# Float32 products of the gated heads' decay and gate rows, replaced by float32r products on stacked rows, in a two-branch recurrent block

## The chip, the cores and the metric

The kernel runs on one core of one Trainium2 chip. The metric is the device time of one execution in microseconds (us); lower is better. A core has five engines with a queue of instructions each: TensorE (PE, matrix products), VectorE (DVE), ScalarE (ACT), GpSimd (POOL) and SyncE (SP, which here issues the loads). Each queue runs in order, and engines wait for each other by semaphores.

## The reference, cut to what matters

One layer: a modulated RMSNorm of 512 latent and 256 context tokens of width 2048, two groups of four heads (gated linear attention, "GLA", and mLSTM) over all tokens in both directions, an output projection, and a gated feed-forward part with a 3x3 convolution. The part that the change touches is the decay of the GLA heads and the gate rows of the mLSTM heads:

```
z = einsum('btd,dp->btp', h, w_in)          # 16 columns are glr, 16 are mgate
dec = einsum('btr,zrk->zbtk', glr, gla_w_lr) + gla_b_lr[:, None, None, :]
gla_loga = log_sigmoid(dec) / 16            # per direction, token, head and 128 channels
pre = mgate.reshape(b, t, 2, 2, 4) + mlstm_b_gate
ml_logi, ml_logf = pre[:, :, :, 0], log_sigmoid(pre[:, :, :, 1])
```

The scans then use the cumulative sums of `gla_loga` within and across chunks. All of it is float32.

## The kernel before, in words

Large products are made exact enough from float32r, a form in which an operand of a product is rounded: each operand is split into a rounded part `hi` and the rest `lo` (`split`: ACT casts, DVE subtracts), and three products are summed (`mm3`, recorded in `mm`, line 95). Small products are plain float32.

The kernel first projects heads 0 and 1 (`project_first`) while the modulation rows `ps_m` are made by products with the loaded `w_mod`. Then come the 32 low-rank rows: `gm` sums them in four strips of 32 partitions, and `small_rows` adds the strips with two products and copies 16 rows to partitions 0 to 15 and 16 rows to 32 to 47 of the tile `glr`, which was set to 1.0 before, so that partition 16 holds ones for the bias.

Then, for each head h, the work of head h (`gla` or `mlstm`, written as generators that yield how many microseconds of other PE work they want) is woven with the projection of head h + 1 (`project_steps`): `weave` takes as many projection steps as the yields ask for. PE's order is pinned to the order of recording, so it is this interleaving that sets what PE does next. In `gla`, nine levels `lv` each make `ex` (DVE differences, ACT exponentials, DVE product with q and k), a product `sl` on PE, and a masked copy of `sl` into `sc` (DVE). After some of these levels, `next(after, None)` records one step of the next head's preparation, `gla_prep(h + 1)`:
- two steps `dec`, one for each direction: PE product of 17 rows, `log_sigmoid` (three ACT operations in `lt`, a DVE operation to `la`);
- two steps `cdec`, for the context tokens: two PE products of 128 columns each, `log_sigmoid` through `ct` to `cla`;
- one step with the scans `bt` (DVE) and the sums `csum` (PE, from `cla`);
- one with `b2` and `ends`.

Head 0's preparation has no levels to stand between and runs in `first_stages` with yields written there. The PSUM tiles of all these small products come from a pool of two (`psb`). After the last GLA head, `ml_gates` picks the gate rows out of `glr` with products by columns of the identity (`pre`), 4 rows for each direction, kinds i and f, latent and context.

Of the kernel before, what the change touches and what calls it, by code (L numbers as in the profile page):

```python
# [11 lines left out]
F32 = mybir.dt.float32  # L12
F32R = mybir.dt.float32r
# [5 lines left out]
P = 128  # L19
# [3 lines left out]
T = 512  # L23
TJ = T // P
TC = 256
CJ = TC // P
H = 4
DK = 128
# [14 lines left out]
C_ID, C_LS, C_US, C_SEG = (P * i for i in range(4))  # L43
C_SA = C_SEG + T
# [25 lines left out]
def block_kernel(ctx: ExitStack, tc: tile.TileContext, a: dict, out: bass.AP):  # L70
    nc = tc.nc
# [22 lines left out]
    def mm(*args, **kw):  # L94
        ins = PE.matmul(*args, **kw)  # L95
        if pinned[0]:
            tc.keep_in_program_order(ins)
# [26 lines left out]
    def cc(off, n=P, p=P):  # L124
        return cst[0:p, off : off + n]
# [270 lines left out]
    st_h = ExitStack()  # L396
    states = pool(st_h, "states")

    glr = states.tile([48, T + TC], F32, name="glr")
# [92 lines left out]
    mskf = mraw.tile([P, len(LEVELS), P], F32, name="mskf", tag="raw")  # L492
    nc.sync.dma_start(mskf, a["masks"])
    V.tensor_copy(msk, mskf)

    V.memset(glr, 1.0)
    gm = [ytile(i, f"gm{i}", (P, n)) for i, n in enumerate((T, TC))]
    pinned[0] = True
    for c0, n, hs, m in ((0, T, hx, gm[0]), (T, TC, hc, gm[1])):
# [11 lines left out]

    def small_rows():
        for c0, n, m in ((0, T, gm[0]), (T, TC, gm[1])):
            ps = psb(f"glr{c0}", (48, n))
            mm(ps[0:16, :], cc(C_SA, 16), m, start=True, stop=True)
            mm(ps[32:48, :], cc(C_SA + 16, 16), m, start=True, stop=True)
            V.tensor_copy(glr[0:16, c0 : c0 + n], ps[0:16, :])
            S.copy(glr[32:48, c0 : c0 + n], ps[32:48, :])
            yield 1.4


# [5 lines left out]
    def wtile(name, tag, *shape):  # L527
        return (wkh if tag in ("qk", "v", "kn", "vn") else wk).tile([P, *shape], F32, name=name, tag=tag)
# [44 lines left out]

    def gla_prep(h, out):

        wlr = wk2.tile([17, 2, DK], F32, name=f"wlr{h}", tag="wlr")
        nc.sync.dma_start(wlr, a["w_lr"][h])
        la = wtile(f"la{h}", "la", 2, T)
        t = wtile(f"lt{h}", "tmp", 2, T)
        cla = wtile(f"cla{h}", "cla", 2, CJ, DK)  # L580
        ct = ytile(15, f"ct{h}", (P, 2, CJ, DK))
# [12 lines left out]
        bt = [ytile(8 + d, f"bt{h}{d}") for d in range(2)]  # L594
        for d in range(2):
            o, x = bt[d], la[:, d]
            if d == 1:
                o, x = o[:, ::-1], x[:, ::-1]
            V.tensor_tensor_scan(out=o, data0=cc(C_SEG, T), data1=x, initial=0.0, op0=ALU.mult, op1=ALU.add)

        ps = psb(f"csum{h}", (P, 2, CJ, DK))
        for d in range(2):
            tri = cc(C_LS) if d == 0 else cc(C_US)
            for j in range(CJ):
                more = j == d
                mm(ps[:, d, j, :], tri, cla[:, d, j, :], start=True, stop=not more)
                if more:
                    mm(ps[:, d, j, :], ones, cla[:, d, 1 - j, :], start=False, stop=True)
# [29 lines left out]
    def gla(h, pair, qk, v, kn, vn, yT, prep, fill, after, pending):  # L638
# [12 lines left out]
        for lv, b in enumerate(LEVELS + [P, 2 * P]):  # L651
# [80 lines left out]
    def ml_gates():  # L732
# [142 lines left out]
    def first_stages(tiles):  # L875

        yield from small_rows()
        prep = gla_prep(0, preps[0])
        for need in (0, 1.4, 0, 3, 1, 0):
            next(prep)  # L880
            yield need
        end = yield from gla(0, *tiles, yT, preps[0], 2.2, gla_prep(1, preps[1]), lambda: None)
        q, k, v0, v1, *c = early_sums
        tiles = ([], (q, k), [v[:, b, :] for v in (v0, v1) for b in range(2)],
                 [e[:, 0:DK] for e in c], [e[:, DK:] for e in c])
        end = yield from gla(1, *tiles, yT, preps[1], 2.2, gla_prep(2, preps[2]), end)
        yield 4
        end()
# [251 lines left out]
def arrange(x, c, ctx, c_ctx, w_mod, b_mod, g_norm1, g_norm2, w_in, gla_w_lr, gla_b_lr, mlstm_b_gate,  # L1140
# [31 lines left out]
    lr = np.concatenate([gla_w_lr[0], gla_b_lr[0][:, None, :]], 1)  # L1172
    r["w_lr"] = lr.reshape(2, 17, H, DK).transpose(2, 1, 0, 3)
    bg = np.zeros((36, 2), np.float32)
    for d in range(2):
        bg[32 * d : 32 * d + H] = mlstm_b_gate[0, d].T
# [25 lines left out]
```

## Time and profile before

| what | value |
|---|---|
| time, median of 3 runs (lowest to highest) | 2604.83 us (2601.96 to 2608.07) |
| the profiled execution: span from first to last instruction | 2605.5 us |
| PE busy | 2543.7 us, 98% |
| DVE busy | 1360.2 us, 52% |
| ACT busy | 875.6 us, 34% |
| mean DMA rate over the span | 123 GB/s |

The profiled execution has no time of its own beside its span; the span lies 0.7 us above the median of the runs. A row of the page's table of groups or of one tile's instructions gives line, engine, operation, output<-inputs, count and durations; a row of the timeline begins with the start and the duration in us, and ends in brackets with the idle time of the engine ahead of it and who ended it. The chain of waits gives start, duration and what the time went to, and merges equal neighbours. A float32 product shows as two records on PE, a float32r product as one.

### The profile page before, as it was taken

To read this page: it belongs to the slowest core of one execution; us is meant where nothing else is said; L and a number is where in the kernel's file an instruction comes from. 1 tells how busy PE (TensorE), PEld (TensorE's weight loads), DVE (VectorE), ACT (ScalarE), POOL (GpSimd) and SP (SyncE) were. 2 spreads that over 40 slices of the span, in tenths; PEclk is the share of its full clock that TensorE was granted. 3 is DMA by queue.
4 is the path that set the end of the run, shared out by engine and by line. 5 is a ranking of instruction groups with operands and counts; after the bars stand their busy time and mean duration, and the time that the engine had idled before them with its cause. 6 is when DMAs were issued, how large, how long until landed. Compare 5 with 4: busy or idle time off the path is not lost.

```text
span 2605.5 us, 31876 instructions
## 1 busy us (share of the span) xinstructions
PE 2543.7 (98%) x12822; PEld 2134.9 (82%) x12822; DVE 1360.2 (52%) x1973; ACT 875.6 (34%) x1300; POOL 226.1 (9%) x179
## 2 busy tenths in 40 slices
PE   5999999999999999999999999999999999999998
PEld 3887889888897887878878888888888888888887
DVE  5566765553434466448586336533653365336643
ACT  4224543332324344334343123312331233123431
POOL 0000000111212323210321000000000000000000
PEclk9999999999999999999999999999999999999999
DMA  8851012222333566642654222322232223222421
GB/s 309 294 194 42 33 41 74 73 79 83 122 122 122 194 228 219 198 139 89 209 180 149 98 96 96 97 97 96 97 97 97 97 97 97 97 97 89 142 89 65
DMA packets 96604, 321.37 MB, mean 123 GB/s; under 512 B 11140, under 2 KB 15560, under 8 KB 96456
## 3 DMA queue, kind: packets, MB, share of 16 engines
q1 hardware_dynamic: 95304, 318.82, 35.7%
q8 instruction: 100, 1.64, 0.3%
q10 hardware_dynamic: 1152, 0.52, 0.1%
q14 instruction: 48, 0.39, 0.0%
HBM read 315.10 MB, written 4.19 MB: 123 GB/s over the span
## 4 chain that ended last, share of the span: by engine, by line
PE 89%; DVE 5%; DMA 4%; ACT 1%; issue 1%; POOL 0%; SPq 0%; DVEq 0%; ACTq 0%; POOLq 0%
PE ug L95 17%; PE a L95 17%; PE dn L95 17%; PE uv L95 16%; PE wo L95 6%; PE ga L95 5%; PE po L95 3%; DMA raw_m<-in_w_mod 3%; PE ps_m L95 1%; PE sl L95 1%; PE dl L95 1%; DVE cv L1038 1%; POOL sum_m L257 0%; PE cst L95 0%; PE s L95 0%
## 5 line engine op out<-in xcount | busy, mean ns | idle before, releaser
L95 PE MATMUL ug<-h2h,hi_ug 128*128 128x512 f32 x688 | 269.0, 392 | 1.6 <-ACT h2h L996 1.6
L95 PE MATMUL uv<-h2h,hi_uv 128*128 128x512 f32 x688 | 267.9, 389 | 1.4 <-ACT hi_uv L89 1.4
L95 PE MATMUL uv<-h2h,lo_uv 128*128 128x512 f32 x688 | 268.0, 390 | 1.1 <-DVE lo_uv L90 1.1
L95 PE MATMUL ug<-h2h,lo_ug 128*128 128x512 f32 x688 | 268.3, 390 | 0.8 <-DVE lo_ug L90 0.8
L95 PE MATMUL ug<-h2l,hi_ug 128*128 128x512 f32 x688 | 268.3, 390 | 0.0
L95 PE MATMUL uv<-h2l,hi_uv 128*128 128x512 f32 x688 | 267.7, 389 | 0.0
L95 PE MATMUL dn<-gh,lo_d 128*128 128x512 f32 x644 | 250.6, 389 | 0.0
L95 PE MATMUL dn<-gh,hi_d 128*128 128x512 f32 x644 | 250.5, 389 | 0.0
L95 PE MATMUL dn<-gl,hi_d 128*128 128x512 f32 x644 | 250.5, 389 | 0.0
L1038 DVE SCALAR_TENSOR_TENSOR cv<-pad,cwt,cv 128x512 f32<-128x512 f32 x344 | 242.6, 763 | 10.6 <-ACT cv L1036 9.2
L90 DVE TENSOR_TENSOR lo_ug<-raw_ug,hi_ug 128x1024 fp32r<-128x1024 f32 (+1 forms) x88 | 107.8, 1225 | 238.4 <-ACT hi_ug L89 238.3
L257 POOL TENSOR_TENSOR sum_m<-sum_m,raw_m 128x512 f32<-128x512 f32 x112 | 174.5, 1558 | 576.0 <-ACT raw_m L256 356.6
L90 DVE TENSOR_TENSOR lo_uv<-raw_uv,hi_uv 128x1024 fp32r<-128x1024 f32 (+1 forms) x88 | 105.5, 1199 | 179.6 <-ACT hi_uv L89 179.1
L90 DVE TENSOR_TENSOR lo_d<-raw_d,hi_d 128x1024 fp32r<-128x1024 f32 x82 | 98.8, 1204 | 166.3 <-ACT hi_d L89 165.2
L255 DVE SCALAR_TENSOR_TENSOR sum_m<-raw_m,csil,sum_m 128x512 f32<-128x512 f32 x112 | 99.8, 891 | 154.1 <-DMA raw_m<-in_w_mod 153.7
L89 ACT CAST hi_ug<-raw_ug 128x1024 fp32r<-128x1024 f32 (+1 forms) x88 | 90.9, 1033 | 263.3 <-PE ug L95 194.1
L89 ACT CAST hi_d<-raw_d 128x1024 fp32r<-128x1024 f32 x82 | 85.0, 1037 | 280.0 <-PE dn L95 231.4
L89 ACT CAST hi_uv<-raw_uv 128x1024 fp32r<-128x1024 f32 (+1 forms) x88 | 90.9, 1033 | 248.6 <-PE uv L95 181.4
L95 PEld LDWEIGHTS ug<-h2h,hi_ug 128*128 128x128 f32 x688 | 129.8, 189 | 28.7 <-ACT h2h L996 1.9
L95 PEld LDWEIGHTS uv<-h2h,lo_uv 128*128 128x128 f32 x688 | 129.1, 188 | 29.2 <-DVE lo_uv L90 2.4
L95 PEld LDWEIGHTS ug<-h2h,lo_ug 128*128 128x128 f32 x688 | 129.6, 188 | 28.3 <-DVE lo_ug L90 1.2
L95 PEld LDWEIGHTS uv<-h2h,hi_uv 128*128 128x128 f32 x688 | 129.1, 188 | 28.4 <-ACT hi_uv L89 1.8
(305 smaller groups left out, 5193.2 us busy)
## 6 DMA issues: line engine op xcount, KB each, us to landing
raw_m<-in_w_mod SPq DMA_DIRECT2D x192, 512.0 KB, 4.3
raw_ug<-in_w_up SPq DMA_DIRECT2D x80, 512.0 KB, 3.2
raw_uv<-in_w_up SPq DMA_DIRECT2D x80, 512.0 KB, 3.2
raw_d<-in_w_down SPq DMA_DIRECT2D x79, 512.0 KB, 3.4
raw_h<-in_w_heads SPq DMA_DIRECT2D x64, 512.0 KB, 3.3
raw_ga<-in_w_gates SPq DMA_DIRECT2D x32, 512.0 KB, 4.1
raw_wo<-in_w_out SPq DMA_DIRECT2D x32, 512.0 KB, 4.5
xl<-in_xT SPq DMA_DIRECT2D x16, 256.0 KB, 5.2
```

The lines of the kernel that those rows point to most:

```text
L89: S.copy(hi, x)
L90: return V.tensor_tensor(out=lo, in0=x, in1=hi.bitcast(F32), op=ALU.subtract).ins
L95: ins = PE.matmul(*args, **kw)
L255: V.scalar_tensor_tensor(out=dv, in0=raw[:, 0, :], scalar=ce, in1=dv, op0=ALU.mult, op1=ALU.add)
L257: G.tensor_tensor(out=po, in0=po, in1=raw[:, 1, :], op=ALU.add)
L1038: V.scalar_tensor_tensor(out=t3, in0=src, scalar=w, in1=t3, op0=ALU.mult, op1=ALU.add)
```

## The change

- The four loads of `wlr` become one load `w3f` of a 128 x 1280 array prepared on the host. ACT casts it to float32r (`w3`), and DVE puts the rest (original minus rounded) on partitions 64 to 95. In the array, the decay weights stand on partitions 0, 32 and 64 onwards, the bias on 80 and 96, and a selection matrix for the gate rows on 16 and 48 onwards.
- `small_rows` makes three products instead of two: the 32 rows on partitions 0 to 31 and again on 32 to 63, the first 16 of them on 64 to 79. ACT casts partitions 0 to 63 to float32r (`g3`), DVE casts 64 to 79, and DVE puts the rest of 32 to 63 there. So one product over 128 contraction rows holds rounded × rounded, rest × rounded and rounded × rest, and the biases.
- `dec` is then one float32r product of 128 rows for each direction, as before one step each.
- The two `cdec` steps become one: for each block of 128 context tokens one float32r product of 256 columns (both directions), and one `log_sigmoid` over 128 x 512 in place of two over 128 x 256. The tiles `cla` and `ct` change their order of axes.
- In `gla`, level 4 no longer calls `next(after)`, since there is one step less; in `first_stages` one yield of 0 goes.
- `pre` becomes one float32r product for each kind and stream (4 instead of 8), with the selection matrix as weights and 128 output rows.

```diff
+    w3f = mraw.tile([P, H * 2 * DK + 2 * P], F32, name="w3f", tag="raw")
+    nc.sync.dma_start(w3f, a["w_lr"])
+    S.copy(w3, w3f)
+    sub(w3[64:96, :], w3f[64:96, :], w3[64:96, :].bitcast(F32))
-    V.memset(glr, 1.0)
+    V.memset(g3[64:P, :].bitcast(F32), 1.0)
...
-            ps = psb(f"glr{c0}", (48, n))
-            mm(ps[0:16, :], cc(C_SA, 16), m, start=True, stop=True)
-            mm(ps[32:48, :], cc(C_SA + 16, 16), m, start=True, stop=True)
-            V.tensor_copy(glr[0:16, c0 : c0 + n], ps[0:16, :])
-            S.copy(glr[32:48, c0 : c0 + n], ps[32:48, :])
+            ps = psb(f"glr{c0}", (80, n))
+            g = g3[:, c0 : c0 + n]
+            mm(ps[0:32, :], cc(C_SA, 32), m, start=True, stop=True)
+            mm(ps[32:64, :], cc(C_SA, 32), m, start=True, stop=True)
+            mm(ps[64:80, :], cc(C_SA, 16), m, start=True, stop=True)
+            S.copy(g[0:64, :], ps[0:64, :])
+            V.tensor_copy(g[64:80, :], ps[64:80, :])
+            sub(g[32:64, :], ps[32:64, :], g[32:64, :].bitcast(F32))
...
-        wlr = wk2.tile([17, 2, DK], F32, name=f"wlr{h}", tag="wlr")
-        nc.sync.dma_start(wlr, a["w_lr"][h])
...
-            mm(ps, wlr[:, d, :], glr[0:17, 0:T], start=True, stop=True)
+            mm(ps, w_lr[:, h, d, :], g3[:, 0:T], start=True, stop=True)
             log_sigmoid(la[:, d], ps, t[:, d])
             yield
-        for d in range(2):
-            ps = psb(f"cdec{h}{d}", (P, CJ, DK))
-            for j in range(CJ):
-                mm(ps[:, j, :], glr[0:17, T + P * j : T + P * j + P], wlr[:, d, :], start=True, stop=True)
-            log_sigmoid(cla[:, d], ps, ct[:, d])
-            yield
+        ps = psb(f"cdec{h}", (P, CJ, 2, DK))
+        for j in range(CJ):
+            mm(ps[:, j], g3[:, T + P * j : T + P * j + P], w_lr[:, h], start=True, stop=True)
+        log_sigmoid(cla, ps, ct)
+        yield
...
-            if lv in (2, 3, 4, 5, 6, 8):
+            if lv in (2, 3, 5, 6, 8):
                 next(after, None)
...
-                ps = psb(f"pre{t}{c0}", (36, n))
-                for d in range(2):
-                    e = C_ID + 32 + 8 * d + 4 * t
-                    mm(ps[rows[d], :], cst[32:48, e : e + H], glr[32:48, c0 : c0 + n], start=True, stop=True)
+                ps = psb(f"pre{t}{c0}", (P, n))
+                mm(ps, w_sel[:, t, :], g3[:, c0 : c0 + n], start=True, stop=True)
...
-        for need in (0, 1.4, 0, 3, 1, 0):
+        for need in (0, 1.4, 3, 1, 0):
```

How the change moves instructions is seen in the built programs; what stands in a row there is line, operation, output<-inputs and the output's shape.

ACT's queue late in the first projection, before: `hi_h` are casts of loaded weights, `rows_m_7` is the copy of the last modulation rows, `hTh` and `hch` are casts of the last activations.

```order
L89 CAST hch_1568<-xc_145 128x256
L89 CAST hi_h_6_1688<-raw_h_6_1687 128x1024
L224 COPY rows_m_7_1732<-ps_m_7_1715 128x256
L89 CAST hi_h_7_1795<-raw_h_7_1794 128x1024
L89 CAST hTh_1751<-xl_137 128x512
```

The same place after:

```order
L89 CAST hi_h_6_1689<-raw_h_6_1688 128x1024
L500 CAST w_91<-w3f 128x1280
L224 COPY rows_m_7_1733<-ps_m_7_1716 128x256
L89 CAST hi_h_7_1796<-raw_h_7_1795 128x1024
L89 CAST hTh_1752<-xl_138 128x512
```

The cast of the stacked weights now stands ahead of the copy of the modulation rows, and its load is released by DVE's cast of the masks (`msk`).

DVE's queue in head 0's preparation, before: `la` and `cla` are the ends of the log-sigmoids, `bt` the scans, `b` the sums over chunks.

```order
L555 SCALAR_TENSOR_TENSOR la_2074<-dec_2078,lt_2075 128x512
L599 SCALAR_TENSOR_TENSOR bt_2128<-cst,la_2074 128x512
L555 SCALAR_TENSOR_TENSOR la_2074<-dec_2084,lt_2075 128x512
L617 COPY b_2153<-bt_2128 128x128
L599 SCALAR_TENSOR_TENSOR bt_2129<-cst,la_2074 128x512
L555 SCALAR_TENSOR_TENSOR cla_2076<-cdec_2102,ct_2077 128x256
L620 TENSOR_SCALAR b_2153<-bt_2128,b_2153 128x128
L617 COPY b_2154<-bt_2129 128x128
L620 TENSOR_SCALAR b_2153<-bt_2128,b_2153 128x128
L620 TENSOR_SCALAR b_2154<-bt_2129,b_2154 128x128
L620 TENSOR_SCALAR b_2153<-bt_2128,b_2153 128x128
L555 SCALAR_TENSOR_TENSOR cla_2076<-cdec_2109,ct_2077 128x256
```

And after:

```order
L565 SCALAR_TENSOR_TENSOR la_2081<-dec_2085,lt_2082 128x512
L565 SCALAR_TENSOR_TENSOR la_2081<-dec_2091,lt_2082 128x512
L606 SCALAR_TENSOR_TENSOR bt_2128<-cst,la_2081 128x512
L606 SCALAR_TENSOR_TENSOR bt_2129<-cst,la_2081 128x512
L624 COPY b_2153<-bt_2128 128x128
L624 COPY b_2154<-bt_2129 128x128
L627 TENSOR_SCALAR b_2153<-bt_2128,b_2153 128x128
L565 SCALAR_TENSOR_TENSOR cla_2083<-cdec_2109,ct_2084 128x512
```

Both `la` now come ahead of both scans, and one `cla`, which `csum` on PE needs, stands where the first of two stood.

PE's queue at level 5 of head 0, where head 1 is prepared, before: `a` are the products of the woven projection, `sl_5` the level's product.

```order
L95 MATMUL a_5_2031<-hi_h_2_2257,hch_740 128x384
L95 MATMUL a_5_2031<-lo_h_2_2258,hch_740 128x384
L95 MATMUL a_5_2031<-hi_h_2_2257,hcl_741 128x384
L95 MATMUL cdec_2364<-wlr_2286,glr 128x128 x2
L95 MATMUL sl_5_2377<-ex_5_2371 128x128 x4
L95 MATMUL a_0_2026<-hTh_931,hi_h_3_2384 128x512
```

And after:

```order
L95 MATMUL a_5_2036<-hi_h_2_2257,hch_741 128x384
L95 MATMUL a_5_2036<-lo_h_2_2258,hch_741 128x384
L95 MATMUL a_5_2036<-hi_h_2_2257,hcl_742 128x384
L95 MATMUL sl_5_2368<-ex_5_2362 128x128 x4
L95 MATMUL a_0_2031<-hTh_932,hi_h_3_2375 128x512
```

The product of the step that was dropped is gone from ahead of `sl_5`; the remaining `cdec` stands ahead of `sl_6`.

More of the change, by code (lines that the diff above doesn't have):

```diff
@@ L397, in block_kernel @@
     states = pool(st_h, "states")
-    glr = states.tile([48, T + TC], F32, name="glr")
+    g3 = states.tile([P, T + TC], F32R, name="g3")
+    w3 = states.tile([P, H * 2 * DK + 2 * P], F32R, name="w3")
+    w_lr = w3[:, 0 : H * 2 * DK].rearrange("p (h d k) -> p h d k", h=H, d=2)
+    w_sel = w3[:, H * 2 * DK :].rearrange("p (t m) -> p t m", t=2)
     acol = states.tile([P, 2, CJ + TJ, H], F32, name="acol")
@@ L574, in gla_prep @@
     def gla_prep(h, out):
-        wlr = wk2.tile([17, 2, DK], F32, name=f"wlr{h}", tag="wlr")
-        nc.sync.dma_start(wlr, a["w_lr"][h])
         la = wtile(f"la{h}", "la", 2, T)
         t = wtile(f"lt{h}", "tmp", 2, T)
-        cla = wtile(f"cla{h}", "cla", 2, CJ, DK)
-        ct = ytile(15, f"ct{h}", (P, 2, CJ, DK))
+        cla = wtile(f"cla{h}", "cla", CJ, 2, DK)
+        ct = ytile(15, f"ct{h}", (P, CJ, 2, DK))
         for d in range(2):
             ps = psb(f"dec{h}{d}")
-            mm(ps, wlr[:, d, :], glr[0:17, 0:T], start=True, stop=True)
+            mm(ps, w_lr[:, h, d, :], g3[:, 0:T], start=True, stop=True)
             log_sigmoid(la[:, d], ps, t[:, d])
             yield
-        for d in range(2):
-            ps = psb(f"cdec{h}{d}", (P, CJ, DK))
-            for j in range(CJ):
-                mm(ps[:, j, :], glr[0:17, T + P * j : T + P * j + P], wlr[:, d, :], start=True, stop=True)
-            log_sigmoid(cla[:, d], ps, ct[:, d])
-            yield
+        ps = psb(f"cdec{h}", (P, CJ, 2, DK))
[3 more added lines that the diff above has]
+        yield
         bt = [ytile(8 + d, f"bt{h}{d}") for d in range(2)]
@@ L605, in gla_prep @@
                 more = j == d
-                mm(ps[:, d, j, :], tri, cla[:, d, j, :], start=True, stop=not more)
+                mm(ps[:, d, j, :], tri, cla[:, j, d, :], start=True, stop=not more)
                 if more:
-                    mm(ps[:, d, j, :], ones, cla[:, d, 1 - j, :], start=False, stop=True)
+                    mm(ps[:, d, j, :], ones, cla[:, 1 - j, d, :], start=False, stop=True)
         kd = ytile(14, f"kd{h}", (P, 2, CJ, DK))
@@ L1171, in arrange @@
     r["w_gates"] = np.stack([blocks(gates[:, 512 * g : 512 * g + 512], 512) for g in range(4)])
-    lr = np.concatenate([gla_w_lr[0], gla_b_lr[0][:, None, :]], 1)
-    r["w_lr"] = lr.reshape(2, 17, H, DK).transpose(2, 1, 0, 3)
+    lr = np.zeros((P, H * 2 * DK + 2 * P), np.float32)
+    w, b = (v.reshape(2, -1, H, DK).transpose(1, 2, 0, 3).reshape(-1, H * 2 * DK) for v in (gla_w_lr[0], gla_b_lr[0]))
+    for p in (0, 32, 64):
+        lr[p : p + 16, : H * 2 * DK] = w
+    for p in (80, 96):
+        lr[p, : H * 2 * DK] = b
+    for t in range(2):
+        for d in range(2):
+            for h in range(H):
+                for p in (16, 48):
+                    lr[p + 8 * d + 4 * t + h, H * 2 * DK + P * t + 32 * d + h] = 1.0
+    r["w_lr"] = lr
     bg = np.zeros((36, 2), np.float32)
```

## Prediction

> **What bounds the kernel now.** I read the page first: the totals of the engines and the chain that ended last.
>
> ```profile
> span 2605.5 us, 31876 instructions
> PE 2543.7 (98%) x12822; PEld 2134.9 (82%) x12822; DVE 1360.2 (52%) x1973; ACT 875.6 (34%) x1300; POOL 226.1 (9%) x179
> PE 89%; DVE 5%; DMA 4%; ACT 1%; issue 1%; POOL 0%; SPq 0%; DVEq 0%; ACTq 0%; POOLq 0%
> ```
>
> TensorE (PE) is busy for 98% of the span and carries 89% of the chain. So a microsecond taken from PE's stream is a microsecond of the end, unless another engine is what PE would then wait for at that place. Which that is, the table by stage shows; the columns are stretch, length, busy time of PE, of its weight loads, of VectorE (DVE), ScalarE (ACT) and GpSimd, then granted clock and DMA.
>
> ```profile
> 208.00:230.00 22.00, 20.27 (x116) 15.60 (x108) 12.15 (x27) 11.23 (x22) 0.00 (x0) 0.92 0.07 23
> 230.00:260.00 30.00, 28.74 (x180) 24.48 (x179) 26.27 (x34) 16.85 (x36) 0.00 (x0) 1.00 0.11 39
> 300.00:314.00 14.00, 13.13 (x76) 10.19 (x75) 12.11 (x19) 10.83 (x24) 0.00 (x0) 1.00 0.12 39
> 370.00:400.00 30.00, 30.00 (x185) 26.54 (x184) 22.57 (x37) 17.73 (x36) 0.73 (x1) 1.00 0.10 36
> ```
>
> The four rows are the four places where the decay of a head is prepared. For head 0 (208 to 230) PE has holes. For head 1 (230 to 260) and head 2 (300 to 314) DVE is busy for 88% and 87% of the time. For head 3 (370 to 400) PE has no hole and DVE has 7 us to spare. The waits of PE in 200 to 515 say who ends the holes (columns: total us, times, longest):
>
> ```profile
> PE sl L95 <- DVE ex L83: 5.9, 4, 3.1
> PE cdec L95 <- DVE la L555: 1.7, 2, 1.1
> PE sl L95 <- DVE la L555: 1.0, 2, 0.7
> PE csum L95 <- DVE cla L555: 0.5, 1, 0.5
> ```
>
> All of them are DVE. That is the question of this change: PE gets less to do at four places, and at three of them DVE is close behind.
>
> **The PE work removed.** The price before is read from the chain of waits around head 3's preparation and around the gate rows, the price after from matmuls of the main projection, which are float32r of the new shapes.
>
> ```profile
> 367.88 1.05 PE dec L95 x2
> 379.90 0.64 PE cdec L95 x4
> 499.44 1.02 PE pre L95 x4
> 506.35 0.53 PE pre L95 x4
> 240.18 0.39 PE L95 MATMUL a<-hTh,lo_h 128*128 128x512 f32 x1
> 240.41 0.39 PE L95 MATMUL a<-hTh,hi_h 128*128 128x512 f32 x1
> 245.76 0.28 PE L95 MATMUL a<-hi_h,hTl 128*128 128x256 f32 x1
> 245.88 0.28 PE L95 MATMUL a<-hi_h,hTh 128*128 128x256 f32 x1
> ```
>
> One `dec` product (float32, two records) takes 1.05 us of PE's time, a pair of `cdec` products 0.64. A float32r product advances the stream by the distance of two starts: 0.23 us for 512 columns, 0.12 for 256. The contraction rows grow from 17 to 128, and the main products have 128 rows too, so this is in the price.
> - Per head two `dec`: 2 × (1.05 − 0.23) = 1.64. Two pairs of `cdec` become one pair of 256 columns: 2 × 0.64 − 2 × 0.12 = 1.04. Together 2.68 us a head, for heads 1, 2 and 3.
> - Gate rows: two `pre` stages of 512 columns and two of 256: 2 × 1.02 + 2 × 0.53 = 3.10, afterwards 2 × 0.23 + 2 × 0.12 = 0.70. Gain 2.4. After them the code asks for 13 us of main products before the next small matmuls, so their results are not needed sooner than before: I book all of it.
> - Head 0's own preparation: its bound is a chain of DVE and ACT, below.
>
> **Head 0's chain.** The chain from `dec` to the first level product `sl`:
>
> ```profile
> 214.69 1.98 PE L95 MATMUL dec<-glr,wlr 17*128 17x512 f32 x4
> 218.15 0.69 DVE L555 SCALAR_TENSOR_TENSOR la<-dec,lt 128x512 f32<-128x512 f32 x1 [4.56 <-ACT lt L554]
> 220.73 0.71 PE L95 MATMUL cdec<-wlr,glr 17*128 17x128 f32 x4 [1.13 <-DVE la L555]
> 226.36 1.23 DVE L90 TENSOR_TENSOR lo_h<-raw_h,hi_h 128x1024 fp32r<-128x1024 f32 x1 [0.66 <-ACT hi_h L89]
> 229.80 2.36 DVE L83 TENSOR_TENSOR ex<-ex,qk 128x1024 f32<-128x1024 f32 x2
> 231.17 1.13 PE L95 MATMUL sl<-ex 128*128 128x128 f32 x8 [0.87 <-DVE ex L83]
> L552 ACT ACTIVATE lt<-dec x8: 579/597/598, 215.8 to 374.6; 128x512 f32<-128x512 f32 x8
> L552 ACT ACTIVATE ct<-cdec x8: 377/384/388, 219.6 to 385.8; 128x256 f32<-128x256 f32 x8
> L555 DVE SCALAR_TENSOR_TENSOR cla<-cdec,ct x8: 399/418/424, 221.9 to 387.2; 128x256 f32<-128x256 f32 x8
> ```
>
> PE waits 0.87 us there for a DVE operation that is the end of an almost unbroken DVE queue from 218.15 on. In that queue the same operations remain. Three things shorten it. The first `la` starts about 0.4 us sooner: `dec` is done some 0.6 sooner, but ACT now does both absolute values and both exponentials ahead of the first logarithm's end, five operations of up to 0.6 where four were. The 0.66 us that DVE waited for `hi_h` goes, since `hi_h` now follows a PE part that starts earlier. Two subtractions of 0.42 become one of 0.69 (the price of `la`), 0.15. Sum 1.2, rounded up to 1.3 with what the earlier `cdec` leaves; bounds 0 (DVE finds a new wait) and 2.68 (all of PE's gain, as in the other heads). PE itself will be ready at about 227.5 and wait for `ex` until about 229.9: the hole gets longer, not shorter.
>
> **Heads 1 and 2, beside a busy DVE.** PE could give 2.68 each. In 230 to 260 DVE is idle for 3.7 us, and those holes are waits for `sl`, which shrink as PE comes earlier. But one step of the preparation is gone from level 4, so `sl` of level 5 comes 1 us sooner while DVE still has `la` and the level's `ex` to do; and the single `cla` follows a longer ACT chain (three operations of 0.6 instead of 0.4) and stands behind one more DVE operation, with `csum` on PE right behind it. Following DVE's queue with these durations I get PE waits of some 1.4 and 1.8 us, and 0.9 of the 2.68 kept; bounds 0 and 2.68. In head 2, DVE's 1.9 idle us in 300 to 314 are what can be had: 1.9; same bounds. In head 3 the whole 2.68, since DVE has 7 us to spare.
>
> **What is added.** A 640 KB load `w3f`, its ACT cast and a DVE subtraction stand late in the first projection. The program lets the load start when DVE's `msk` cast is done, and ACT's in-order queue then has the cast of `w3f` ahead of a copy of modulation rows that PE needs:
>
> ```profile
> 170.72 0.63 DVE L494 CAST msk<-mskf 128x896 uint8<-128x896 f32 x1 [0.47 <-DMA mskf<-in_masks]
> raw_h<-in_w_heads SPq DMA_DIRECT2D x2, 512.0 KB, 3.1
> mskf<-in_masks SPq DMA_DIRECT2D x1, 448.0 KB, 7.7
> 175.79 0.37 ACT L224 COPY rows_m<-ps_m 128x256 f32<-128x256 f32 x1 [7.91 <-PE ps_m L95]
> 176.77 0.50 PE L95 MATMUL ps_m<-cst,rows_m 128*128 128x2 f32 x4
> 177.01 1.05 ACT L89 CAST hi_h<-raw_h 128x1024 fp32r<-128x1024 f32 x1 [0.84 <-PE a L95]
> 208.12 0.69 PE L95 MATMUL gm<-hcl,wsm 128*32 128x256 f32 x8
> 212.52 0.61 PE L95 MATMUL glr<-gm,cst 128*16 128x256 f32 x4
> ```
>
> Start 171.4. The row nearest in time is the 3.1 us of 512 KB loads on the quiet queue at 172 to 178; with a quarter more bytes I take 3.6. It lands at 175.0, the cast takes 1.05 × 1280/1024 = 1.3, the copy is done at 176.7, just when PE asks. The DVE subtraction (1.23 × 1.25 = 1.5) pushes `e`, `shcol` and the modulation behind it by 0.8, about the slack it has. I book 0.3 of loss. Bounds 0, and by the crowded 7.7: landing 179.1, copy done 180.8, 4.0 us of PE wait. SP's next load waits for a later DVE operation and isn't held up; the four small loads `wlr` go.
> The low-rank rows `glr` become three products instead of two, in three column strips. Eight records in the four strips of `gm` take 0.69, four in two strips of `glr` 0.61, so strips run side by side: I take 0.1 (bounds 0 and 0.9, a third product after the others: half of 0.61, and twice that for 512 columns). Its copies and the new subtraction end before `dec` asks for them at 214.7.
>
> **The sum.** 1.3 + 0.9 + 1.9 + 2.7 + 2.4 − 0.3 − 0.1 = 8.8 us. The profiled execution's span is 2605.5, 0.7 above the median 2604.8 of the runs. I take the gain from the median: 2596.0. (From the span it would be 2596.7.) About 0.2%, 5.2 us, is what can be told from no change.
>
> **The clock.** A longer hole in PE can cost more than its length:
>
> ```profile
> 222.00:225.00 3.00, 3.00 (x11) 3.00 (x10) 3.00 (x14) 1.37 (x3) 0.00 (x0) 0.50 0.03 9
> 455.00:460.00 5.00, 3.33 (x24) 3.10 (x24) 5.00 (x7) 1.48 (x3) 1.11 (x1) 1.00 0.43 139
> 460.00:465.00 5.00, 1.87 (x13) 1.70 (x12) 4.74 (x5) 1.82 (x4) 0.65 (x1) 0.91 0.47 168
> 465.00:470.00 5.00, 5.00 (x32) 5.00 (x31) 2.88 (x4) 3.24 (x10) 1.38 (x1) 0.74 0.03 12
> ```
>
> After head 0's two waits for `la` (1.7 us together) the granted clock is 0.50 for some 3 us. After the hole of 3.1 us in 460 to 465 it falls too: 0.91 and 0.74 over 5 us each are (0.45 + 1.3) / 0.5 = 3.5 us at half clock. A hole of 1.67 us in 455 to 460 left it at 1.00. One spell costs half its 3.5 us, about 1.7. [...]
>
> **The rivals.**
> - *DVE sets the end in all three near-bound stages.* Then head 0, 1 and 2 give nothing and head 3 and the gates are left: 2.7 + 2.4 − 0.4 = 4.7, time 2600.1. For it: 26.27 of 30; against it: DVE's idle time there is waiting for PE. 0.20.
> - *PE keeps everything.* 4 × 2.68 + 2.4 − 0.4 = 12.7, time 2592.1. Against it: the DVE rows. 0.13.
> - *The load of the stacked weights is late*, as the `mskf` load was: 3.7 us more loss, time 2599.7. 0.10.
> - *Half clock after new holes*: slower. By hand I find up to eight new or longer PE holes of 1.4 to 2.4 us. If each brought a spell at 0.50, that is 8 × 1.7 = 13.6 against 8.8: time 2609.6. Up to five spells leave a gain, from six on it is a loss; slower by over 0.2% takes all eight and a little more. Against it: the 455 to 460 row. 0.05.
> - *The removed float32 products were hidden anyway*: no change, 2604.8. Against it: 30.00 of 30.00 PE in head 3. 0.03.
>
> The forecast has 0.49. The range 2591 to 2603.5 takes in the bounds of the first four cases (12.7 of gain to one of 1.3); outside are the last two and some of the edges. Faster by over 0.2%: nearly all of the forecast, the full gain, and a third of the DVE and late-load cases, 0.66; within: 0.30; slower 0.04.
>
> **What would show it.** `dec` in starts of 0.23 and two records of `cdec` a head; PE busy down by about 12 us; longer waits of PE for `ex` before the first `sl`, and a new wait of `csum` for `cla` in head 1; no hole at 177. I am wrong if `ps_m` waits for `rows_m` by more than 1 us, if the clock falls in 230 to 320, or if head 3's stage is shortened by less than 2.5 us.

## The result, and the profile after

| kernel | median | lowest to highest | ratio to before, 95% interval |
|---|---|---|---|
| before (9 runs) | 2606.93 us | 2601.96 to 2608.59 | |
| changed (9 runs) | 2598.28 us | 2592.77 to 2605.71 | 0.9965 [0.9952, 0.9977] |

The change made the kernel 8.65 us faster by the medians; 8.8 were forecast. The profiled execution has a span of 2597.0 against 2605.5. The page's totals and its shares of the chain that ended last:

```profile
span 2597.0 us, 31782 instructions
PE 2530.0 (97%) x12782; PEld 2132.0 (82%) x12782; DVE 1361.3 (52%) x1972; ACT 873.7 (34%) x1289; POOL 225.8 (9%) x179
PE 89%; DVE 5%; DMA 3%; issue 1%; ACT 1%; SPq 0%; POOL 0%; DVEq 0%; ACTq 0%; POOLq 0%
```

PE is busy for 13.7 us less than before, and only 8.5 of them left the span. The table by stage, same four stretches and columns as in the prediction (stretch, length, busy time of PE, weight loads, DVE, ACT, GpSimd, then granted clock and DMA):

```profile
208.00:230.00 22.00, 16.73 (x104) 13.37 (x99) 15.24 (x30) 11.40 (x20) 0.00 (x0) 0.99 0.08 25
230.00:260.00 30.00, 27.11 (x173) 25.08 (x173) 26.39 (x36) 17.18 (x34) 0.00 (x0) 0.95 0.11 36
300.00:314.00 14.00, 10.34 (x62) 9.29 (x61) 12.28 (x18) 9.37 (x22) 0.00 (x0) 0.91 0.12 39
370.00:400.00 30.00, 30.00 (x198) 28.02 (x197) 21.47 (x34) 17.33 (x33) 0.73 (x1) 1.00 0.17 53
```

In the first three PE is idle for 5.3, 2.9 and 3.7 us (before: 1.7, 1.3, 0.9), while DVE has as much or more to do there (15.24, 26.39 and 12.28 for 12.15, 26.27 and 12.11), and the clock is down to 0.95 and 0.91; before, it was down in the first (0.92, now 0.99). Only the last, head 3's preparation, has no hole in either kernel. The waits of PE in 200 to 515 name who ended the holes (total us, times, longest):

```profile
PE sl L95 <- DVE ex L83: 12.3, 7, 3.1
PE cdec L95 <- DVE la L565: 1.8, 1, 1.8
PE csum L95 <- DVE b L624: 1.6, 1, 1.6
PE csum L95 <- DVE cla L565: 1.3, 1, 1.3
```

Before, `sl` waited 5.9 us for `ex`. So about 8 us of the PE time set free became waiting for DVE. The chain of waits in head 3's preparation shows the price of the new products (start, duration, what):

```profile
367.41 0.24 PE dec L95
367.65 0.89 PE sl L95 x8
...
372.03 0.23 PE dec L95
372.26 0.89 PE sl L95 x8
...
381.77 0.24 PE cdec L95 x2
382.01 0.89 PE sl L95 x8
```

`dec` went from 1.05 to 0.23 and two pairs of `cdec` of 0.64 to one of 0.24, as booked. Not booked: the `sl` right behind them went from 1.09 (at 368.93 before) to 0.89.

Five marks on PE's timeline cut the changed part into stages: the first `dec`, head 0's first `sl`, the `sd` that opens head 2's and head 3's `gla`, the first `pre`, the first `pa`. In the changed kernel (start, duration, ..., idle before in brackets; of `pa` it is 514.44):

```profile
213.76 0.63 PE L95 MATMUL dec<-g,w 128*128 128x512 f32 x2
228.98 1.40 PE L95 MATMUL sl<-ex 128*128 128x128 f32 x8 [2.19 <-DVE ex L83]
343.62 0.61 PE L95 MATMUL sd<-qk 128*128 128x128 f32 x4
430.19 1.06 PE L95 MATMUL sd<-qk 128*128 128x128 f32 x8
494.33 0.50 PE L95 MATMUL pre<-g,w 128*128 128x512 f32 x1 [0.34 <-ACT yT L582]
```

The differences of such starts, for every kernel of this study (us):

| kernel | dec to first sl | to head 2's sd | to head 3's sd | to pre | to pa | dec to pa |
|---|---|---|---|---|---|---|
| before | 16.48 | 112.91 | 90.08 | 65.28 | 23.00 | 307.75 |
| before again (e12) | 16.24 | 112.88 | 90.07 | 65.61 | 23.03 | 307.83 |
| changed | 15.22 | 114.64 | 86.57 | 64.14 | 20.11 | 300.68 |
| changed again (e1) | 15.21 | 112.97 | 86.58 | 65.50 | 20.11 | 300.37 |
| changed, third (e11) | 15.91 | 111.44 | 86.58 | 65.39 | 20.11 | 299.43 |
| float32, one log-sigmoid (e2) | 15.10 | 113.15 | 88.46 | 66.67 | 22.04 | 305.42 |
| float32, two cdec steps (e6) | 16.09 | 111.46 | 88.48 | 65.68 | 22.04 | 303.75 |
| float32r, two cdec steps (e3) | 14.65 | 109.76 | 86.79 | 65.56 | 20.11 | 296.87 |
| the same again (e8) | 14.66 | 109.78 | 86.78 | 65.65 | 20.11 | 296.98 |
| one cdec step, at level 4 (e7) | 15.61 | 110.03 | 86.61 | 66.53 | 20.11 | 298.89 |
| before with one log-sigmoid (e5) | 15.22 | 114.24 | 89.64 | 65.51 | 23.03 | 307.64 |
| changed, steps moved (e4) | 16.23 | 112.98 | 86.57 | 65.34 | 20.11 | 301.23 |
| two steps, moved (e9) | 14.82 | 109.55 | 86.79 | 65.37 | 20.11 | 296.64 |
| two steps, one earlier (e10) | 14.81 | 111.66 | 86.79 | 64.66 | 20.11 | 298.03 |

The stage "to head 2's sd" holds the work of heads 0 and 1 and the preparation of heads 1 and 2; "to head 3's sd" the preparation of head 3; "to pa" the gate rows. The same kernel repeats from the first `dec` to the first `pa` within 1.3 us, while whole runs of one kernel differ by up to 13. So the change's own gain is read here: 307.8 to 300.2 on the mean of the traces, 7.6 us.

A single stage has to be read together with the clock that was granted in the same trace. In places it falls to 0.50 for 3.4 us (in the changed kernel from 229.69 to 233.10 and from 311.62 to 315.03), here called a spell at half clock, and the spells stand in different stages of different traces. The table counts them by stage. The last two columns split the stage "to head 2's sd" at the `sd` that opens head 1's `gla`, so the first part holds the preparation of head 1 and the second that of head 2 (us).

| kernel | spells to first sl | spells to head 2's sd | spells to pre | head 1's part | head 2's part |
|---|---|---|---|---|---|
| before, and e12 | 1 | 0 | 1 | 50.97, 50.98 | 61.94, 61.90 |
| changed | 0 | 2, one in each part | 0 | 51.39 | 63.25 |
| changed again (e1) | 0 | 1, in head 1's part | 1 | 51.37 | 61.60 |
| changed, third (e11) | 1 | 0 | 1 | 49.84 | 61.60 |
| e2 | 0 | 0 | 2 | 50.88 | 62.27 |
| e6 | 1 | 0 | 1 | 50.22 | 61.24 |
| e3, and e8 | 1 | 0 | 1 | 49.13, 49.13 | 60.63, 60.65 |
| e7 | 1 | 1, in head 2's part | 1 | 48.61 | 61.42 |
| e5 | 0 | 0 | 1 | 51.61 | 62.63 |
| e4 | 0 | 2, in head 2's part | 1 | 49.82 | 63.16 |
| e9 | 0 | 1, in head 1's part | 1 | 49.41 | 60.14 |
| e10 | 0 | 1, in head 2's part | 1 | 48.81 | 62.85 |

The stage "to head 2's sd" as a stretch, with the columns of the table by stage, for the kernel before, the changed kernel's first and third trace (e11), and e5:

```profile
231.17:344.08 112.91, 110.62 (x664) 97.50 (x665) 85.44 (x152) 59.03 (x126) 0.00 (x0) 1.00 0.09 30
228.98:343.62 114.64, 107.59 (x649) 98.71 (x650) 85.77 (x150) 57.84 (x120) 0.00 (x0) 0.97 0.09 29
230.59:342.03 111.44, 104.42 (x649) 95.57 (x649) 85.62 (x150) 57.84 (x120) 0.00 (x0) 1.00 0.09 30
229.06:343.30 114.24, 110.19 (x656) 96.86 (x657) 85.84 (x150) 59.36 (x122) 0.00 (x0) 1.00 0.09 29
```

PE's idle time in it, the length less the busy time, is 2.3 us before and 7.0 in both traces of the changed kernel. The 3.2 us between these two are busy time at half clock: 1.6 a spell. At full clock the stage went from 112.9 to 111.4. In head 0's chain, where PE waits for DVE at the end anyway, a spell costs less: the changed kernel takes 15.2 without one and 15.91 with one. From `dec` to `pa` there are two spells in each trace of both kernels, so the 7.6 us compare like with like in their number, though not in their place.

### The profile page after: what moved, and what is told of

Same layout as the page of the kernel before. It is cut to its first block, busy times and chain, and to the rows that moved or that the text cites. A ratio compares the mean times of both kernels' runs of the same rounds, so it can differ in the third digit from the quotient of the medians.

```text
span 2597.0 us, 31782 instructions
## 1 busy us (share of the span) xinstructions
PE 2530.0 (97%) x12782; PEld 2132.0 (82%) x12782; DVE 1361.3 (52%) x1972; ACT 873.7 (34%) x1289; POOL 225.8 (9%) x179
## 3 DMA queue, kind: packets, MB, share of 16 engines
q8 instruction: 100, 1.64, 0.3%
## 4 chain that ended last, share of the span: by engine, by line
PE 89%; DVE 5%; DMA 3%; issue 1%; ACT 1%; SPq 0%; POOL 0%; DVEq 0%; ACTq 0%; POOLq 0%
PE ug L95 18%; PE uv L95 17%; PE dn L95 17%; PE a L95 16%; PE wo L95 6%; PE ga L95 5%; PE po L95 3%; DMA raw_m<-in_w_mod 2%; PE sl L95 1%; PE dl L95 1%; PE ps_m L95 1%; DVE cv L1043 1%; DMA raw_h<-in_w_heads 1%; PE s L95 0%; PE cst L95 0%
```

## The experiments

**What repeats (e1, e11, e12).** The changed kernel twice more, and the kernel before once more.

> The changed kernel once more, to see which stage lengths repeat. From first gm to first dec, from dec to head 0's first sl, from there to head 1's last sl, and so on, each stage should repeat within about 0.5 us if it was set by the program; the 0.8 us that the first trace was ahead before any changed operation, and the 1.15 us in 450 to 470, should not repeat if they are chance. Time about 8.5 us below the kernel before.

> The changed kernel a third time, as the measure for the two others on this chip: 300 to 301 from the first dec to the first pa, the two-step kernels 4 to 7 below; in time 2 to 4 us above them if the yardstick is right, equal to them if what is gained there is given back behind it.

> The kernel before once more, since all stage lengths of before come from one trace. If they are the program's: dec to head 0's sl 16.5, from there to head 2's sd 112.9, head 2's sd to head 3's sd 90.1, first pre to first pa 23.0, each within 0.3 us; first dec to first pa 307 to 308.5. If the start (gm at 200.8) and the part behind pa belong to the program, they repeat within 0.5 us as well; if they are chance, they do not.

Measured: e1 2593.89 us, 0.9954 [0.9941, 0.9968]; e11 2596.93, 0.9957 [0.9944, 0.9971]; e12 one run, 2607.14. By the medians these two lie 12.6 and 10.0 us below the kernel before on their chips. The stages of the changed kernel repeat within 0.1 us where the spells stand alike, and otherwise not within the 0.5 that was expected. Outside them nothing can be told from chance: the first `gm` starts at 200.78 and 201.24 in the two traces of before, at 199.52, 199.94 and 200.86 in those of the changed kernel, and 199.94 in e5, which is the kernel before up to there. From the first `pa` to the end of the span it is 2083.1 and 2082.4 us before, 2082.6, 2079.2 and 2082.5 changed. So the 0.84 us that the first trace of the changed kernel was ahead at `gm`, and the differences behind `pa`, are no larger than what the same kernel shows from trace to trace. The 1.15 us in 450 to 470 did not repeat either: the stage "to pre" is 65.5 and 65.4 in e1 and e11, which have a spell at half clock there, as before has; the first trace has none.

**The form of the product alone (e2).** Same stacked operands and steps, float32 instead of float32r.

```diff
-            mm(ps, w_lr[:, h, d, :], g3[:, 0:T], start=True, stop=True)
+            mm(ps, w_lr[:, h, d, :].bitcast(F32), g3[:, 0:T].bitcast(F32), start=True, stop=True)
... likewise for cdec and pre
```

> The changed kernel with dec, cdec and pre as float32 products of the same stacked operands (same rows, same steps, one log-sigmoid; only the form of the product differs). Cover theory (the PE time freed in the stages of heads 0 and 1 became holes in front of DVE and ACT, so those stages gave nothing): from head 0's first sl to the csum of head 2's preparation (about 229 to 317) within 1 us of the changed kernel, with smaller PE holes; head 3's stage about 3.5 us and the pre stage about 2.4 us longer, head 0's chain up to 1.3; in all 6 to 7 us slower than the changed kernel, 2 faster than before. Rival (PE keeps everything): all 12.7 us of freed PE time come back, time at or above that of the kernel before.

Measured: 2600.19 us, 0.9974 [0.9964, 0.9985]; 6.3 us above e1 on the same chip. From `dec` to head 2's `sd` it takes 128.25 us against 128.18 in e1 and 127.4 to 129.9 in the three traces of the changed kernel, so by its number the cover theory holds. But e2 has no spell at half clock in that part and each of the others has one or two. At full clock the stage to head 2's `sd` is 113.15 with float32 and 111.44 with float32r (e11): the faster product bought 1.7 us there, and half clock took it back, nearly all of it in e1 and more than that in the first trace. Head 3's stage is 1.9 us longer and the gate rows 1.9. The rival (all 12.7 come back) falls. The chain of waits of this kernel in head 3's preparation:

```profile
365.30 0.86 PE dec L95 x2
366.16 0.89 PE sl L95 x8
...
380.92 0.86 PE cdec L95 x4
381.78 0.89 PE sl L95 x8
```

A float32 `dec` over 128 rows takes 0.86 us and the `sl` behind it 0.89; over 17 rows it was 1.05 and 1.09. So part of the gain of head 3 is from the rows, not from the form: 90.08 to 88.46 with float32 over 128 rows, then to 86.57 with float32r.

**Two cdec steps again (e3, e8).** The one log-sigmoid is undone, all else as in the changed kernel.

```diff
+        for d in range(2):
+            ps = psb(f"cdec{h}{d}", (P, CJ, DK))
+            for j in range(CJ):
+                mm(ps[:, j, :], g3[:, T + P * j : T + P * j + P], w_lr[:, h, d, :], start=True, stop=True)
+            log_sigmoid(cla[:, :, d, :], ps, ct[:, :, d, :])
+            yield
...
-            if lv in (2, 3, 5, 6, 8):
+            if lv in (2, 3, 4, 5, 6, 8):
```

> The changed kernel with two cdec steps as before (float32r, one log-sigmoid for each direction, the step after level 4 again). Cover theory: DVE has as much to do as with one log-sigmoid and one operation more, the holes only move; time within 1.5 us of the changed kernel. Rival (the merged log-sigmoid, with its longer ACT chain and the missing step at level 4, made the waits of csum and sl): the waits of PE in head 1's and head 2's preparation fall from about 8 us to under 4, and the time is 3 to 4 us below the changed kernel.

> The two-step float32r kernel once more. If its 125.0 in the stage of heads 0 and 1 is the program's, it repeats within 0.5 us. If its late start (gm at 201.0 where four others had 199.4 to 200.0) was chance, gm comes at 199.4 to 200.0 and the time is 2 to 3 us below the changed kernel's, about 2591 on the chip of the first four runs; if it belongs to the program, gm is late again and the time equals the changed kernel's.

Measured: 2594.13 us, 0.9949 [0.9936, 0.9961], and 2592.90, 0.9950 [0.9938, 0.9962]. From `dec` to `pa` 296.9 and 297.0, 3.2 us below the mean of the changed kernel, in both traces: that is the rival's size. Against e11, which has its spells in the same stages, it is 2.5: 1.3 in head 0's chain (15.91 to 14.65), 0.7 in head 1's part and 1.0 in head 2's, less 0.2 each in head 3's stage and "to pre". In whole runs it looks like the first theory (within 1.5 us), since 0.9950 is not told from 0.9954 to 0.9965 with intervals of some 0.0013 to each side. The runs scatter by more than the 3.2 us in question and the stages don't, so I go by the stages: the merge made a part of the waits. Of e8's expectation, the start came late again (`gm` at 200.69), but so it did in the third trace of the changed kernel. The waits of PE in 200 to 515 of e8:

```profile
PE sl L95 <- DVE ex L83: 7.4, 6, 3.1
PE cdec L95 <- DVE la L565: 2.0, 2, 1.8
PE sl L95 <- DVE la L565: 1.3, 1, 1.3
PE sl L95 <- DVE cla L565: 0.8, 1, 0.8
```

Of the 17 us of the changed kernel 11.5 are left, and the two waits of `csum` are gone from the top. (One of the two, the 1.3 us for `cla`, stands in head 0's chain, and in e11 it is gone as well, with the spell that stands there.)

**Is it the merge itself? (e5, e6, e7).** Three kernels: the kernel before with only the merge; float32 over stacked rows with two steps; the changed kernel with its one step a level sooner (`if lv in (2, 3, 4, 6, 8)`).

```diff
 # e5, in the kernel before
+        ps = psb(f"cdec{h}", (P, CJ, 2, DK))
+        for j in range(CJ):
+            mm(ps[:, j], glr[0:17, T + P * j : T + P * j + P], wlr, start=True, stop=True)
+        log_sigmoid(cla, ps, ct)
```

> The kernel before with only the one log-sigmoid of the context tokens (float32 products over 17 rows as before, both directions in one product of 256 columns, one cdec step, none after level 4). Stage of heads 0 and 1, from the first dec to head 2's sd: 129.4 us in the kernel before, 128.2 to 129.9 in the changed one, 125.0 with two cdec steps and the rest changed. Theory (the merge costs about 3 us there whatever the products' form): 132 to 133, time 2 to 3 us slower than before. Rival (the merge costs only where PE has been made faster): 129 to 130, time equal to before within 1 us.

> Stacked rows as in the changed kernel, but float32 products and two cdec steps. Theory (in the stage of heads 0 and 1 the form of the product is worth nothing, since DVE and ACT set its length): first dec to head 2's sd within 1 us of the 125.0 of the two-step float32r kernel; head 3's stage about 2 us and the gate rows 2.1 us longer than there; 4 to 5 us slower than that kernel. Rival (without the merge PE is near the bound and the form counts): 127 to 128.5 in that stage, 7 us slower.

> The changed kernel with its one cdec step a level sooner (steps after levels 2, 3, 4, 6, 8 instead of 2, 3, 5, 6, 8). Theory of place (the merged chain is not too long in itself, it only starts too late for csum): the waits of csum and of the sl after it shrink, first dec to head 2's sd 125 to 126.5, 2 to 3 us faster than the changed kernel. Rival (the longer chain of ACT and DVE costs what it costs): the wait moves to the sl of levels 4 and 5, stage 128 to 130, no gain.

Measured: e5 2607.34 us, 1.0006 [0.9996, 1.0017]; e6 2601.34, 0.9980 [0.9972, 0.9989]; e7 2594.82, 0.9958 [0.9946, 0.9970]. From `dec` to `pa`, and in the stage to head 2's `sd` at full clock, the two halves of the change cross (us; the changed kernel's 300.2 is the mean of its three traces, its 111.4 is e11's):

| products | two steps, dec to pa | one log-sigmoid, dec to pa | the merge costs | two steps, to head 2's sd | one log-sigmoid, to head 2's sd | the merge costs there |
|---|---|---|---|---|---|---|
| float32, 17 rows | 307.8 | 307.6 | −0.2 | 112.9 | 114.2 | 1.3 |
| float32, 128 rows | 303.8 | 305.4 | 1.7 | 111.5 | 113.2 | 1.7 |
| float32r, 128 rows | 296.9 | 300.2 | 3.2 | 109.8 | 111.4 | 1.7 |

In both e5 and e6 the rival's number held. In e6 its reason holds too: without the merge the form counts (127.55 from `dec` to head 2's `sd` in e6, 124.4 in e3, with the spells in the same stages). In e5 it does not. Its −0.2 is a sum that hides the cost: 1.0 to 1.3 are gained in head 0's chain, where before has a spell at half clock and e5 has none, and 0.4 in head 3's stage.

In the stage of heads 1 and 2, where none of the traces of the last three columns has a spell, the merge costs 1.3 to 1.7 us with every form of the products, half of what the theory named, and the faster products gain 2.8 us with the merge and 3.1 without. In head 0's chain the merge costs 1.3 with float32r; with float32 no two traces there have the same clock.

In e7 the theory of place held: 125.6 from `dec` to head 2's `sd`, although it has a spell in each of the two stages. Head 1's part, which has none, is 48.61 where the step at level 5 has 49.84, and the wait of `csum` in it is gone:

```profile
PE sl L95 <- DVE ex L83: 9.7, 6, 3.1
PE cdec L95 <- DVE la L565: 1.8, 1, 1.8
PE sl L95 <- DVE la L565: 1.3, 1, 1.3
PE cdec L95 <- DVE sc L690: 0.5, 1, 0.5
```

In whole runs the 2 to 3 us are not to be seen. Its trace lost 1.0 against e1 in the stage "to pre", at the same clock (0.97), where PE waited 1.42 us ahead of one `sl` for `ex` and 0.39 in e1; why, stays open. So the merged chain is not too long in itself; after level 5 it starts too late for `csum`. Why, the timelines of ACT, DVE and PE in the changed kernel show, for head 1's preparation (start, duration, engine, line, operation):

```profile
253.16 2.44 ACT L677 ACTIVATE ex<-b,ends 128x128 f32<-128x128 f32 x8
255.74 0.60 ACT L562 ACTIVATE ct<-cdec 128x512 f32<-128x512 f32 x1
256.37 0.63 ACT L563 ACTIVATE ct<-ct 128x512 f32<-128x512 f32 x1
256.91 0.49 ACT L677 ACTIVATE ex<-b,ends 128x256 f32<-128x256 f32 x1
257.31 0.62 ACT L564 ACTIVATE ct<-ct 128x512 f32<-128x512 f32 x1
...
254.86 2.33 DVE L606 TENSOR_TENSOR_SCAN bt<-cst,la 128x512 f32<-128x512 f32 x2
257.11 1.20 DVE L83 TENSOR_TENSOR ex<-ex,qk 128x1024 f32<-128x1024 f32 x1
258.23 0.72 DVE L690 COPY_PREDICATED sc<-msk,sl 128x512 f32<-128x512 uint8 x1
258.84 0.68 DVE L565 SCALAR_TENSOR_TENSOR cla<-cdec,ct 128x512 f32<-128x512 f32 x1
...
259.67 1.58 PE L95 MATMUL csum<-cla,cst 128*128 128x128 f32 x12 [1.64 <-DVE b L624]
```

When the step after level 5 starts, ACT already has the exponentials of levels 7 and 8, which are many small operations; the merged chain stands among them, and its `cla` on DVE behind both scans, one `ex` and one copy. It ends at 259.5 and `csum` starts at 259.67, after a wait of 1.64. (The profile names the neighbour `b`; `csum` reads `cla`, which ends just then.) With two steps the first direction's `cla` starts at 254.34 and the second's at 257.78.

**Moving the projection steps instead (e4, e9, e10).** The same products, woven differently: more where PE waited, fewer where it was full.

```diff
 # e4
-        for need in (0, 1.4, 3, 1, 0):
+        for need in (0, 2.8, 4.2, 1, 2):
-        end = yield from gla(0, ..., 2.2, ...)
+        end = yield from gla(0, ..., [2.2, 2.2, 1.6, 1.6, 2.2, 3.4, 2.2, 3.2, 1.2, 1.0], ...)
-        end = yield from gla(1, ..., 2.2, ...)
+        end = yield from gla(1, ..., [2.2, 2.2, 2.2, 1.6, 1.6, 3.2, 3.2, 1.6, 0.6, 0.6], ...)
 # e9 and e10, on the two-step kernel: needs (0, 2.8, 0, 3, 1, 1) and [2.2] * 8 + [1.2, 1.0] for head 0; needs (0, 2.8, 0, 3, 1, 0)
```

> The changed kernel with the same projection steps woven otherwise into the stages of heads 0 and 1: more of them at the places where PE waited (head 0's preparation: needs 0, 2.8, 4.2, 1, 2; after levels 4 and 6 of head 0, after 4 and 5 of head 1), fewer after levels 1, 2, 7 and 8. Cover theory with half clock after holes: the holes between 212 and 317 fall from 13 us to under 8 and the granted clock there stays above 0.97; 3 to 6 us faster than the changed kernel. Rival (DVE and ACT set the length of the two stages wherever PE's work stands): the holes move to the places that lost steps, time within 1 us of the changed kernel.

> The two-step float32r kernel with 1.4 us more of projection steps after head 0's second dec and 1 us before its first level (needs 0, 2.8, 0, 3, 1, 1), and 2.2 us fewer after head 0's levels 7 and 8, where PE had no hole. From the first dec to the first pa: 307.8 us in the kernel before, 300.5 in the changed one, 296.9 in the two-step kernel. Theory (a hole of about 1.8 us in front of cdec and the half clock behind it cost that kernel some 3 us, and steps can be taken where PE is full): 293 to 295, time 2 to 3 us below the two-step kernel. Rival (the chain of DVE and ACT through heads 0 and 1 sets the length, as it did when the steps of the changed kernel were moved): 296.5 to 298, no gain.

> The two-step float32r kernel with only the 1.4 us more after head 0's second dec; head 1's last steps then run out 1.4 us sooner. Theory: the hole in front of cdec falls from 1.8 to under 0.7, the granted clock in 217 to 226 stays at 1.00, first dec to first pa 294.5 to 296. Rival: head 0's first sl comes no sooner, since the queue of DVE sets it, and what was moved is missing behind head 1's last level: 296.5 to 298.

Measured: e4 2600.01 us, 0.9972 [0.9962, 0.9983]; e9 2591.75, 0.9942 [0.9929, 0.9954]; e10 2596.43, 0.9954 [0.9942, 0.9967]. From `dec` to `pa` e4 takes 301.2 (changed: 300.2), e9 296.6 and e10 298.0 (two steps: 296.9): by its number the rival held all three times (e4's whole runs are even 6 us above e1's, with intervals that touch). The lists of waits show where the holes went; the first two rows of e4 in 200 to 345:

```profile
PE yt L100 <- DVE ob L575: 2.6, 2, 1.4
PE sl L95 <- DVE ex L83: 2.4, 2, 2.2
```

The holes ahead of `sl` shrank, and new ones of 2.6 us came where head 1's work ends and its last projection steps were missing (2.5 in e10). Heads 0 and 1 share one projection, so a step can be used once. Half clock has a part in it: e4 has two spells in a row at the new holes (336.1 to 342.9; over 300 to 343 the clock was 0.92), and e9 and e10 have one in the stage to head 2's `sd`, where the two-step kernel has none. So what moving the steps is worth at the same clock stays open. In e9 and e10 the added step landed behind `cdec`, not ahead of it, because steps come whole; the wait of `cdec` stayed at 1.80, so these two say nothing about that wait. e9 has the lowest median of the study and beats the kernel before, but its interval overlaps that of e11 on the same chip (0.9957), and in the stages it is the two-step kernel.

## Why the prediction was right, point by point

The time was right (2598.3 for 2596.0, inside 2591 to 2603.5), and the sum for the part from `dec` to `pa` was 9.2 (1.3 + 0.9 + 1.9 + 2.7 + 2.4) where 7.6 was measured. Of its terms, those of head 0 and head 1 held, head 0's with some luck; that of head 2 failed; those of head 3 and the gate rows were too small.

- *Head 0's own chain, 1.3*: 1.26, 1.27 and 0.57 against the 16.48 of the first trace. Part of it is luck: both traces of before have a spell at half clock here, and of the changed kernel only the one with 0.57 has. The reason given (a chain of DVE and ACT, not PE's time) fits: with one log-sigmoid and no spell the chain is 15.1 to 15.2 us whatever the products are (e2, e5, the changed kernel). That two steps would have kept more here (14.65 in e3 and e8, with a spell) was not foreseen.
- *Heads 1 and 2, 0.9 and 1.9*: head 1's term held at full clock and head 2's failed. Head 1's part went from 50.97 to 49.84 (e11), 1.1; with a spell at half clock it is 51.4. Head 2's went from 61.94 to 61.60 (e1 and e11, full clock), 0.3. The step that failed is the reading that DVE's 1.9 us of idle time in 300 to 314 are what can be had there: the prediction priced the step gone from level 4 and the longer chain in head 1 (1.8 of the 2.68) and not at all in head 2. The runs showed in its place that PE waits for `ex` ahead of two `sl` of head 2's part, by 1.78 and 1.88 us; before, two waits there took 0.65 (for `la`) and 0.22. Over both parts PE's busy time fell by 6.2 us, its idle time rose by 4.7, and 1.5 were kept. Without the merge (e3, e8) head 2's part gains 1.3 and both together 3.1; with the one step at level 4 (e7) both gain 2.9 in spite of a spell. On the mean of the three traces both parts together gave −0.1 for the 2.8: the other 1.6 went to half clock. So the rival that DVE sets the end holds nearly for head 2 in the kernel as changed, and the place of a step has a part in that.
- *Head 3, 2.7*: 3.5. The term missed that the `sl` behind each 17-row product became shorter too, four times 0.2 us, which is the difference. It was all kept, since PE has no hole there.
- *Gate rows, 2.4*: 2.9, from the first `pre` to the first `pa`. The price of the new products was right; the 0.5 beyond it fits the neighbours of the products over few rows, as in head 3: with float32 over 128 rows (e2) the stage is already 1.0 shorter, and six main products behind a `pre` take 1.38 us there and 1.57 before.
- *Load, −0.3, and third strip, −0.1*: nothing. `w3f` landed in 4.0 us, and PE's wait at `ps_m` went from 0.3 to 0.4; from `gm` to `dec` it takes 13.8 us for 13.9. The late load did not happen. Both rows are of the changed kernel, from its DMA issues and its waits:

```profile
w3f<-in_w_lr SPq DMA_DIRECT2D x1, 640.0 KB, 4.0
PE ps_m L95 <- DVE e L329: 0.4, 1, 0.4
```

- *Half clock after new holes*: in the first trace it came true in small. One of the conditions named for being wrong was met: the clock fell in 230 to 320. Stretches of the changed kernel behind the holes ahead of head 0's first and head 1's level-6 `sl`:

```profile
226.00:229.00 3.00, 0.81 (x5) 0.36 (x3) 2.90 (x5) 2.27 (x4) 0.00 (x0) 1.00 0.04 14
229.00:232.00 3.00, 3.00 (x17) 3.00 (x18) 2.89 (x5) 0.00 (x0) 0.00 (x0) 0.62 0.00 0
232.00:235.00 3.00, 3.00 (x23) 3.00 (x23) 1.89 (x3) 0.96 (x2) 0.00 (x0) 0.82 0.00 0
...
311.00:314.00 3.00, 2.50 (x12) 2.52 (x13) 2.07 (x4) 1.25 (x4) 0.00 (x0) 0.60 0.00 0
314.00:317.00 3.00, 3.00 (x21) 3.00 (x21) 3.00 (x11) 1.20 (x3) 0.00 (x0) 0.83 0.00 0
```

In the first pair (0.38 + 0.18) × 3 / 0.5 = 3.4 us at half clock, in the second the same: 1.7 us each, the price that the prediction gave a spell, twice and not eight times. They explain why the first trace has 114.6 in this stage, e1, without the second, 113.0, and e11, with neither, 111.4. From `dec` to `pa` before has two spells as well, so the spells of the changed kernel stand elsewhere, in the first trace both in this stage, but there are no more of them.

So that the total came out this near is in part luck: the overrated heads 1 and 2 (2.8 forecast, −0.1 on the mean) stood beside two underrated terms (by 0.8 and 0.5) and 0.4 of loss that did not come, and the medians of the first comparison hold 1 us more than the stages show, those of e1 and e11 2 to 5 us more; where that lies is not shown.

## What to carry to other kernels

A microsecond taken from the busiest engine was a microsecond of the end only where that engine had no hole (of 13.7 us less PE time 8.5 left the span); read the busy time and the waits stage by stage and book each stage by itself. When a step of a chain is merged with its neighbour, ask which slot of the schedule it now starts in and who stands ahead of it in each queue there: here one log-sigmoid for two cost 1.3 to 1.7 us in the stage of heads 1 and 2, whatever the form of the products, and a slot one level sooner took it back (head 1's part 48.6 us against 49.8, and 49.1 without the merge). And when runs scatter more than the effect, compare the starts of a few named instructions within one execution: here they repeated to 1.3 us where the runs scattered by 13. Read the granted clock of each stage beside its length first: two spells at half clock made one stage 3.2 us longer, and without that reading the merge seemed free with the slow products.

## What the runs showed of the hardware that was not expected

- The float32 product over few rows was dearer than over all: `dec` of 512 columns took 1.05 us over 17 rows and 0.86 over 128, and the float32 `sl` behind it 1.09 and 0.89.
- A hole of the same length was followed by half clock in one execution and not in the next. The changed kernel waited 1.78 and 1.88 us ahead of two `sl` and ran at 0.60 in 311 to 314; in e1 the waits were 1.79 and 1.85, and the clock stayed at 1.00:

```profile
311.00:314.00 3.00, 2.95 (x24) 2.98 (x25) 2.89 (x5) 2.02 (x5) 0.00 (x0) 1.00 0.00 0
314.00:317.00 3.00, 3.00 (x26) 3.00 (x25) 2.53 (x15) 0.67 (x2) 0.00 (x0) 1.00 0.00 0
```

The same with `cdec` after a wait of 1.80 us: in 220 to 223 the clock was 0.57 in e8 and 1.00 in e10. In the changed kernel a wait of 2.19 us ahead of head 0's first `sl` had a clock of 0.62 behind it, in 229 to 232. What decides whether a spell comes is not shown.
